# A planner's price for transfers: one rate for the whole run, and a later due time for the rows of x in the output stage

## The chip, the cores and the metric

The kernel runs on one core of a Trainium2 chip. The metric is the time of one execution on the device in microseconds (us), lower is better. Three runs of the kernel before gave 2049.25, 2057.58 and 2060.75 us; their median, 2057.58 us, is the time before.

## What is computed

One layer of a streaming encoder runs over 2048 prompt frames and, with caches, over 32 sample frames; the model width D is 1024. Two branches read the same normalised rows h: A is attention over a band of nine chunks of 64 frames (8 heads of 64), B is a gated delta rule (8 heads of 64) in its exact chunked form. Cut to what matters:

```python
h = layer_norm(x, ln0_g, ln0_b)
qa, ka, va, za, qkv_b, zb, a_b, b_b, gate_a, gate_b = split(h @ w_in)      # 1024 x 6160
oa = softmax(qa @ band(ka).T * 64**-0.5 + rel_bias) @ band(va)
ya = (oa * silu(za)) @ w_branch_a
c  = silu(causal_conv(qkv_b, conv_w))                                      # width 4
q, k, v = l2norm(c_q) * 64**-0.5, l2norm(c_k), c_v
g, beta = -exp(a_log) * softplus(a_b + dt_bias), sigmoid(b_b)
# per head and chunk of 64 frames, with decay from cumsum(g):
M = strict_lower((beta * k) @ k.T * decay);  T = inverse(I + M)
u, w = T @ (beta * v), T @ (beta * k * exp(gc))
v_new = u - w @ S;  o = (q * exp(gc)) @ S + (q @ k.T * decay) @ v_new
S = S * exp(g_last) + (k * exp(g_last - gc)).T @ v_new                     # chunk after chunk
yb = (rms_norm(o) * gdn_norm_w * silu(zb)) @ w_branch_b
mix = sigmoid(gate_a) * ya + sigmoid(gate_b) * yb
y = layer_norm(2**0.25 * h + mix @ w_out, ln_g, ln_b)
```

The last keys and values, the last three rows before the convolution and the state S are outputs too. Wide products are made exact enough by splitting each operand into a high and a low part and adding three products (high by high, low by high, high by low).

## The kernel before

**Stages.** The prompt is worked in two halves of 1024 frames (the sample frames ride with the second). Per half, phase B (delta rule) comes first, then phase A (attention). Under both runs one stream of projection jobs: one job is 128 columns of `w_in` times all frames of the half, and its matmuls write the PSUM tile `pj`. The jobs fill TensorE between the short dependent matmuls of the phases. When the second half's jobs are used up, a last stage multiplies the gated branch outputs (`glo`, `ghi`) by the branch weights (PSUM tile `a`, three banks), multiplies by the gate rows (`sg`, read back from `sig`), adds the branches, splits the sum into `mh` and `ml`, multiplies by `w_out` (`woh`, `wol`; PSUM tiles `pj` and `b`), adds a row block of x (`xt`), and normalises. That stage goes through eight blocks of 256 frames.

**The delta rule's solve.** A system is eight chunks of one pair of heads; there are 17. Its matrix leaves as `sol_p<-p_c` (four transfers), comes back spread as `sys_p<-sol_p` (four), VectorE solves it by substitution in 62 short instructions on `sys_t` and `sys_u`, the result leaves as `sol_u<-sys_u` (four), comes back as `tu<-sol_u`, VectorE transposes it (`tu_t`), and TensorE completes the inverse (`b<-tu_t,p_c`). After that the recurrence runs on TensorE and VectorE in turn (`x<-state,k_bd`, `r`, `x<-r,u_bd`, `vn`, `x<-vn,kd_bd`, `state`).

**What sets the order.** The program is written by a planner that runs while the kernel is built. Each piece of work is a Python generator (a stream) with its own clock. `Flow.run` always advances the stream with the smallest clock, and each instruction that a stream issues adds a price (`Engine.price`) to that clock and to its engine's. The order in which the planner issues is the order of the instructions on each engine, and on the chip each engine keeps that order. All transfers are issued by SyncE (SP), in that same order. The planner prices a transfer in `Flow.transfer` (line 204): the issue takes 0.5 us, data moves one transfer after another through a single resource `"DMA"` at `size / rate`, and 1.6 us (`MARGIN`) is added. A stream that yields the returned time goes on only when the planner's clock has got there. So the price of a transfer decides how far down each engine's queue its first user stands; on the chip that user still waits for the real landing. The rate is 360e3 bytes per us for transfers that start before the planner's 25 us, and 200e3 after that. Sizes are counted with at least 768 bytes for each contiguous run (line 291).

**Lines of the steps.** `transfer` 204 to 211, `dma` 283 to 292, `solve` 1255, `inverse` 1291, `last_weights` 2006 (loads of `w_out`, each started 5 us, `LEAD`, before the landing planned for the one before), `load_g` 2071 (`glo`), `merge` 2093, `sg_ahead` 2189, `x_load` 2212, `finish` 2230. Nearly every recorded instruction has line 262, the wrapper's; its tiles tell which it is.

Of the kernel before, what the change touches and what calls it, by code (L numbers as in the profile page):

```python
# [21 lines left out]
P = 128  # L22
# [133 lines left out]
class Flow:  # L156
# [47 lines left out]
    def transfer(self, queue, size):  # L204

        start = max(self.cur.clock + 0.2, self.busy.get(queue, 0.0)) + 0.5
        self.busy[queue] = start

        end = max(start + 0.6, self.busy.get("DMA", 0.0)) + size / (360e3 if start < 25.0 else 200e3)
        self.busy["DMA"] = end  # L210
        return end + MARGIN

# [58 lines left out]
def trunk(ctx: ExitStack, tc: tile.TileContext, x_p, x_s, cache_k, cache_v, st_conv, st_gdn,  # L271
# [11 lines left out]
    def dma(dst, src, eng=nc.sync):  # L283

        eng.dma_start(dst, src)  # L285
        size = 2 if dst.dtype == F16 else 4
        n = size
        for k in dst.shape:
            n *= k

        n = max(n, n // (size * dst.shape[-1]) * 768)
        return flow.transfer("SP" if eng is nc.sync else "S", n)
# [7 lines left out]
    def mark():  # L300
        return Mark(flow)
# [1902 lines left out]
    def x_ahead():  # L2204
        n = SEQ // P
        for gt in [*range(n - 2), n, n - 2, n - 1]:
            yield x_slots
            w = Rows()
            flow.start(x_load(w, gt, P if gt < SEQ // P else DEC))
            q_x[gt == SEQ // P].put(w)  # L2210

    def x_load(w, gt, rows):
        w.ready, w.half_done = mark(), mark()
        w.xt = xt = fp.tile([P, D], F32, tag="xt", bufs=3, name="xt")
        w.st = fp.tile([P, 2, 6], F32, tag="fst", bufs=3, name="fst")
        yield dma(xt[:rows], x_s if rows < P else x_p[gt * P:(gt + 1) * P, :])
        yield rows_ready
        V.tensor_scalar(out=xt[:rows], in0=xt[:rows], scalar1=mv[:rows, gt, 0:1],
                        scalar2=mv[:rows, gt, 1:2], op0=ALU.subtract, op1=ALU.mult)
        yield  # L2220
        eng = V if gt < 2 else G

        for name, op in (("l0g", ALU.mult), ("l0b", ALU.add)):
            for q in range(4):
                cs = slice(q * 256, (q + 1) * 256)
                eng.tensor_tensor(out=xt[:rows, cs], in0=xt[:rows, cs], in1=rowv[name][:rows, cs], op=op)
            yield
        w.ready.done()
# [130 lines left out]
```

## Time and profile before

| | |
|---|---|
| runs | 2049.25, 2057.58, 2060.75 us |
| profiled execution | 2061.14 us, of which the span of the instructions is 2059.3 us |
| mean granted clock of TensorE | 0.983 of full speed |
| TensorE matmuls busy | 1977.9 us, 96% of the span |
| VectorE, ScalarE, GpSimd busy | 1454.2, 976.6, 711.3 us |
| transfers | 196.55 MB, mean 95 GB/s |

Busy time is the time in which at least one instruction of the engine is recorded as running. Phase B of the first half lies at about 100 to 480 us, phase A at 480 to 800, the second half's phase B at 900 to 1290 and phase A at 1290 to 1655. At 1655 to 1750 the projections end and the output stage begins; from 1750 to 2000 it runs evenly.

### The profile page before, as it was taken

How to read it: one execution, taken by the hardware profiler on the slowest of the kernel's cores; microseconds unless marked ns; L12 is line 12 of the kernel's file. 1: busy time of each engine (PE TensorE's matmuls, PEld its weight loads, DVE VectorE, ACT ScalarE, POOL GpSimd, SP SyncE). 2: the span in 40 equal slices, each digit the busy share in tenths (PEclk: the TensorE clock that was granted, in tenths of full speed). 3: DMA queues.
4: the chain of work that ended last, by engine and by line, in shares of the span. 5: the costliest groups of instructions: out<-in, count | busy, mean ns of one | idle time of the engine just before them, and what ended most of it. 6: DMA issues, size and time to landing. Idle time of an engine off the chain costs nothing. (4 is left out here: it accounts for less than half of the span.)

```text
span 2059.3 us, 42008 instructions
## 1 busy us (share of the span) xinstructions
PE 1977.9 (96%) x15157; PEld 1422.6 (69%) x15157; DVE 1454.2 (71%) x4674; ACT 976.6 (47%) x2098; POOL 711.3 (35%) x1075
## 2 busy tenths in 40 slices
PE   8999999999999998998999999999999998999998
PEld 5455666666466656565767777766776687999996
DVE  7788888773478757679988886356757677655665
ACT  6665455444466667564544544356656551111110
POOL 6444343333312123344243442311111134643453
PEclk9999999999999999999999999999999999999999
DMA  4223332332333233223232233332233355433331
GB/s 139 65 85 108 94 89 71 84 104 80 112 90 116 68 94 89 66 81 84 66 80 78 78 104 86 105 92 75 75 95 92 94 161 179 135 103 122 104 125 47
DMA packets 198745, 196.55 MB, mean 95 GB/s; under 512 B 80642, under 2 KB 148590, under 8 KB 198536
## 3 DMA queue, kind: packets, MB, share of 16 engines
q1 hardware_dynamic: 198536, 193.86, 32.0%
q8 instruction: 120, 1.97, 0.4%
q14 instruction: 89, 0.73, 0.1%
HBM read 135.91 MB, written 50.53 MB: 91 GB/s over the span
## 5 line engine op out<-in xcount | busy, mean ns | idle before, releaser
L262 PE MATMUL pj<-hi,whi 128*128 128x512 f16 (+2 forms) x1992 | 649.9, 341 | 11.9 <-ACT sig L262 3.2
L262 PE MATMUL pj<-hi,wlo 128*128 128x512 f16 (+2 forms) x1952 | 641.7, 341 | 0.5 <-POOL wlo L262 0.5
L262 PEld LDWEIGHTS <-whi 128*128 128x128 f16 x3984 | 412.3, 105 | 212.9 <-issue 8.3
L262 PE MATMUL pj<-lo,whi 128*128 128x512 f16 (+2 forms) x1992 | 459.9, 338 | 0.0
L262 POOL TENSOR_TENSOR wlo<-wraw,whi 128x256 f16<-128x256 f32 x384 | 265.1, 712 | 555.5 <-ACT whi L262 305.5
L262 PEld LDWEIGHTS <-wlo 128*128 128x128 f16 x1952 | 206.3, 106 | 113.6 <-issue 11.2
L262 ACT CAST mh<-sg 128x256 fp32r<-128x256 f32 x64 | 26.0, 407 | 275.4 <-DVE sg L262 275.4
L262 ACT ACTIVATE wraw<-wraw,w_scale 128x1024 f32<-128x1024 f32 (+1 forms) x98 | 111.6, 1139 | 58.5 <-DVE w_scale L262 54.3
L262 PE MATMUL a<-ghi,whi 128*128 128x256 f32 (+1 forms) x512 | 132.3, 289 | 6.8 <-DVE sg L262 6.6
L262 ACT CAST ph<-b 128x512 f16<-128x512 f32 (+2 forms) x224 | 92.6, 422 | 91.9 <-PE b L262 87.0
L262 PE MATMUL a<-ghi,wlo 128*128 128x256 f32 (+1 forms) x512 | 130.5, 286 | 1.1 <-DVE wlo L262 1.1
L262 DVE TENSOR_TENSOR sys_u<-sys_u,sys_t 128x60 f32<-128x60 f32 (+23 forms) x527 | 125.5, 242 | 7.8
L262 ACT CAST whi<-wraw 128x512 f16<-128x512 f32 (+1 forms) x196 | 119.3, 611 | 24.2 <-PE pj L262 21.4
L262 DVE TENSOR_TENSOR pl<-b,ph 128x512 f16<-128x512 f32 (+2 forms) x224 | 106.8, 484 | 30.4 <-ACT ph L262 29.3
L262 ACT ACTIVATE sb<-sb,mx,unit 128x640 f32<-128x640 f32 (+4 forms) x128 | 108.9, 851 | 22.9 <-DVE mx L262 22.4
L262 DVE SCALAR_TENSOR_TENSOR acc<-raw,cwT,acc 128x512 f32<-128x512 f32 x144 | 113.5, 789 | 7.7 <-ACT acc L262 6.5
L262 DVE TENSOR_TENSOR sys_t<-sys_u,sys_p 128x60 f32<-128x60 f32 (+21 forms) x459 | 111.0, 243 | 6.5
L262 POOL TENSOR_TENSOR w_scale<-w_scale,mhalf 128x1 f32<-128x1 f32 x49 | 30.0, 612 | 245.2 <-DVE w_scale L262 181.0
L262 ACT COPY v_t<-o 128x64 f32<-128x64 f32 x132 | 27.6, 209 | 163.4 <-PE o L262 124.2
L262 PEld LDWEIGHTS a<-ghi,whi 128*128 128x128 f32 x512 | 97.9, 191 | 9.2 <-DVE sg L262 8.8
L262 PE MATMUL b<-ident,sb 128*128 128x128 f32 x560 | 99.4, 277 | 2.5 <-DVE ga L262 1.4
L262 DVE CUSTOM_DVE_ANT_0 sb<-a,bias 128x320 f32<-128x320 f32 (+4 forms) x128 | 61.7, 486 | 54.2 <-PE a L262 53.7
(353 smaller groups left out, 4288.8 us busy)
## 6 DMA issues: line engine op xcount, KB each, us to landing
wraw<-in_w_in SPq DMA_DIRECT2D x192, 256.0 KB
sg<-sig SPq DMA_DIRECT2D x112, 128.0 KB
sig<-sig SPq DMA_DIRECT2D x44, 256.0 KB
sys_p<-sol_p SPq DMA_DIRECT2D x68, 128.0 KB
x<-in_x_p SPq DMA_DIRECT2D x16, 512.0 KB
xt<-in_x_p SPq DMA_DIRECT2D x16, 512.0 KB
out_y_p<-xt SPq DMA_DIRECT2D x16, 512.0 KB
glo<-g SPq DMA_DIRECT2D x14, 512.0 KB
```

Of the source, the lines that this page charges most:

```text
L262: r = f(*a, **k)
```

## The change

Two edits. `Flow.transfer` counts every transfer at 360e3 bytes per us, whenever it starts. `x_load` adds 3.0 us to the planned landing of each row block of x, before its first use. Every engine keeps the same number of instructions; what changes is their order.

```diff
--- before.py
+++ after.py
@@ -206,7 +206,7 @@
         start = max(self.cur.clock + 0.2, self.busy.get(queue, 0.0)) + 0.5
         self.busy[queue] = start
 
-        end = max(start + 0.6, self.busy.get("DMA", 0.0)) + size / (360e3 if start < 25.0 else 200e3)
+        end = max(start + 0.6, self.busy.get("DMA", 0.0)) + size / 360e3
         self.busy["DMA"] = end
         return end + MARGIN
 
@@ -2213,7 +2213,8 @@
         w.ready, w.half_done = mark(), mark()
         w.xt = xt = fp.tile([P, D], F32, tag="xt", bufs=3, name="xt")
         w.st = fp.tile([P, 2, 6], F32, tag="fst", bufs=3, name="fst")
-        yield dma(xt[:rows], x_s if rows < P else x_p[gt * P:(gt + 1) * P, :])
+
+        yield dma(xt[:rows], x_s if rows < P else x_p[gt * P:(gt + 1) * P, :]) + 3.0
         yield rows_ready
         V.tensor_scalar(out=xt[:rows], in0=xt[:rows], scalar1=mv[:rows, gt, 0:1],
                         scalar2=mv[:rows, gt, 1:2], op0=ALU.subtract, op1=ALU.mult)
```

**VectorE, the first solve of the run.** `tu_t<-tu` opens the inverse of the first system; the rows on `sys_t` and `sys_u` are the substitution of the second one, and the last number of their shape falls by one from step to step. Before:

```order
L262 TENSOR_TENSOR sys_t<-sys_u,sys_p 128x4x18
L262 RECIPROCAL w_half<-w_scale 128x1
L262 TENSOR_TENSOR qk_bd_739<-b,e_in 64x4x64 x2
L262 SCALAR_TENSOR_TENSOR acc<-raw_2128,cwT,acc 128x512
L262 TENSOR_TENSOR sys_u<-sys_u,sys_t 128x4x18
L262 TENSOR_SCALAR w_inv<-w_half,h_scale 128x1
L262 TENSOR_SCALAR w_half<-w_half,h_scale 128x1
L262 STREAM_TRANSPOSE tu_t<-tu 128x256
L262 TENSOR_TENSOR sys_t<-sys_u,sys_p 128x4x17
```

After:

```order
L262 TENSOR_TENSOR sys_t<-sys_u,sys_p 128x5x15
L262 TENSOR_SCALAR w_scale<-w_scale 128x1
L262 TENSOR_TENSOR p_c_768<-b,gcb 128x256
L262 TENSOR_TENSOR sys_u<-sys_u,sys_t 128x5x15
L262 RECIPROCAL w_half<-w_scale 128x1
L262 STREAM_TRANSPOSE tu_t<-tu 128x256
L262 TENSOR_TENSOR qk_bd_739<-b,e_in 64x4x64 x2
L262 TENSOR_TENSOR sys_t<-sys_u,sys_p 128x5x14
```

The second system's substitution is three steps further along where the first system's result is taken up. On TensorE the first `b<-tu_t,p_c` stands 60 matmuls earlier in the program than before (the 893rd and not the 953rd), and the later ones of the first half 71 to 133 earlier.

**SyncE, where the output stage begins.** `l0g`, `l0b`, `lng`, `lnb` are the vectors of the two norms spread over 128 partitions (512 KB each) when they come from `in_ln`, and buffers for pieces of `w_out` when they come from `in_w_out`. `xt` is 512 KB of x, `glo` the gated outputs of block 1, `sg<-sig` gate rows (here `sig_74`, `sig_75`, `sig_82`, `sig_83` belong to block 0, the others to block 1). Before:

```order
L285 DMA glo<-g_66 128x4x256
L285 DMA glo<-g_67 128x4x256
L285 DMA lng<-in_w_out 128x512
L285 DMA sg<-sig_69 128x256
L285 DMA sg<-sig_77 128x256
L285 DMA sg<-sig_70 128x256
L285 DMA sg<-sig_78 128x256
L285 DMA lng<-in_w_out 128x512
L285 DMA l0g<-in_ln_g 128x1024
L285 DMA l0b<-in_ln_b 128x1024
L285 DMA xt<-in_x_p 128x1024 x3
L285 DMA lng<-in_ln_g 128x1024
```

After:

```order
L285 DMA sg<-sig_74 128x256
L285 DMA l0g<-in_ln_g 128x1024
L285 DMA sg<-sig_82 128x256
L285 DMA l0b<-in_ln_b 128x1024
L285 DMA sg<-sig_75 128x256
L285 DMA xt<-in_x_p 128x1024 x2
L285 DMA sg<-sig_83 128x256
L285 DMA xt<-in_x_p 128x1024
L285 DMA lng<-in_ln_g 128x1024
L285 DMA glo<-g_66 128x4x256
L285 DMA glo<-g_67 128x4x256
L285 DMA sg<-sig_68 128x256
```

The norm's vectors and the rows of x have moved ahead of everything of block 1, and in between the last gate rows of block 0.

**VectorE at the same place.** `xt<-xt,mv` is the first use of a row block of x, `glo<-glo,ghi` the split of block 1's input, `sg<-sg,a` empties a bank of `a`. Before:

```order
L262 TENSOR_TENSOR glo<-glo,ghi 128x256 x4
L262 TENSOR_TENSOR wol_22609<-lng,woh_22588 128x512
L262 TENSOR_SCALAR xt<-xt,mv 128x1024
L262 TENSOR_TENSOR xt<-xt,l0g 128x256 x4
L262 TENSOR_SCALAR xt<-xt,mv 128x1024
L262 TENSOR_TENSOR xt<-xt,l0b 128x256 x4
L262 TENSOR_TENSOR xt<-xt,l0g 128x256 x4
L262 TENSOR_SCALAR xt<-xt,mv 128x1024
L262 SCALAR_TENSOR_TENSOR xt<-pj,xt 128x512
```

After:

```order
L262 SCALAR_TENSOR_TENSOR sg<-sg,a 128x256 x2
L262 TENSOR_TENSOR sg<-sg 128x256
L262 TENSOR_SCALAR xt<-xt,mv 128x1024
L262 TENSOR_TENSOR xt<-xt,l0g 128x256 x4
L262 TENSOR_SCALAR xt<-xt,mv 128x1024
L262 TENSOR_TENSOR xt<-xt,l0b 128x256 x4
L262 TENSOR_SCALAR xt<-xt,mv 128x1024
L262 TENSOR_TENSOR xt<-xt,l0g 128x256 x4
L262 TENSOR_TENSOR glo<-glo,ghi 128x256 x2
L262 SCALAR_TENSOR_TENSOR xt<-pj,xt 128x512
L262 TENSOR_TENSOR glo<-glo,ghi 128x256 x2
```

The split of block 1's input has moved from before the rows of x to behind them. The two passes `xt<-xt,m,lng` and `xt<-xt,m,lnb` of the first row block, which stood behind block 1's first `sg<-sg,a`, now stand ahead of it.

## Rows read from the trace of the kernel before

**Rows 1.** The page: the span, and busy time by engine.

```profile
span 2059.3 us, 42008 instructions
PE 1977.9 (96%) x15157; PEld 1422.6 (69%) x15157; DVE 1454.2 (71%) x4674; ACT 976.6 (47%) x2098; POOL 711.3 (35%) x1075
```

**Rows 2.** Windows: stretch, busy PE, PEld, DVE, ACT, POOL (count), clock, DMA share, GB/s.

```profile
100.00:480.00 380.00, 364.29 (x2641) 238.65 (x2639) 312.95 (x1147) 194.03 (x386) 148.66 (x250) 0.97 0.33 91
...
800.00:900.00 100.00, 92.02 (x721) 64.03 (x722) 68.06 (x141) 61.01 (x117) 39.37 (x63) 0.97 0.22 68
900.00:1290.00 390.00, 374.56 (x3210) 281.32 (x3209) 326.84 (x1187) 181.83 (x406) 143.37 (x254) 0.98 0.30 83
...
1655.00:1750.00 95.00, 85.01 (x617) 75.35 (x615) 70.20 (x150) 30.28 (x68) 39.58 (x39) 0.95 0.53 170
1750.00:2000.00 250.00, 250.00 (x1578) 227.20 (x1577) 147.62 (x276) 33.18 (x91) 115.67 (x148) 1.00 0.37 116
```

**Rows 3.** Waits of PE: total us, times, longest.

```profile
PE a L262 <- DVE sg L262: 6.6, 7, 2.3
...
PE x L262 <- DVE state L262: 4.0, 8, 0.9
PE x L262 <- DVE r L262: 3.7, 12, 0.7
PE x L262 <- DVE vn L262: 3.4, 9, 1.1
...
PE x L262 <- DVE sys_t L262: 2.8, 2, 2.3
```

**Rows 4.** Timeline of SP, first solve (start us, us, engine, line, op, tiles).

```profile
124.77 1.85 SPq L285 DMA_DIRECT2D sys_p<-sol_p  x4
...
177.59 0.51 SPq L285 DMA_DIRECT2D tu<-sol_u  x1
```

**Rows 5.** Tile sys_p and timeline of DVE: first uses in the first solve.

```profile
L262 DVE TENSOR_SCALAR sys_t<-sys_p,sys_u x68: 221/240/687, 135.0 to 1244.7; 128x31 f32<-128x31 f32 x17, 128x30 f32<-128x30 f32 x17, 128x29 f32<-128x29 f32 x17, 128x28 f32<-128x28 f32 x17
...
197.56 0.43 DVE L262 STREAM_TRANSPOSE tu_t<-tu 128x256 f32<-128x256 f32 x1
```

**Rows 6.** Timeline of SP at the start of the output stage.

```profile
1703.27 0.96 SPq L285 DMA_DIRECT2D l0g<-in_ln_g  x1
1704.27 0.44 SPq L285 DMA_DIRECT2D l0b<-in_ln_b  x1
1704.75 1.64 SPq L285 DMA_DIRECT2D xt<-in_x_p  x3
```

**Rows 7.** Timeline of DVE there; in brackets idle time before, and what ended it.

```profile
1702.58 3.42 DVE L262 TENSOR_TENSOR glo<-glo,ghi 128x256 fp32r<-128x256 f32 x4
...
1712.98 0.81 DVE L262 TENSOR_SCALAR xt<-xt,mv 128x1024 f32<-128x1024 f32 x1 [5.26 <-DMA xt<-in_x_p]
...
1727.14 0.41 DVE L262 SCALAR_TENSOR_TENSOR sg<-sg,a 128x256 f32<-128x256 f32 x1
...
1728.07 1.27 DVE L262 SCALAR_TENSOR_TENSOR xt<-xt,m,lng 128x1024 f32<-128x1024 f32 x1
```

**Rows 8.** Timeline of PE there.

```profile
1727.60 0.39 PE L262 MATMUL a<-ghi,whi 128*128 128x256 f32 x1 [2.32 <-DVE sg L262]
...
1744.92 0.39 PE L262 MATMUL a<-ghi,whi 128*128 128x256 f32 x1 [1.42 <-DVE sg L262]
```

**Rows 9.** The chain of waits: start us, us, what.

```profile
1704.75 8.14 DMA xt<-in_x_p
...
1749.46 5.48 PE pj L262 x24
...
1771.30 22.77 PE a L262 x192
```

**Rows 10.** Windows of 10 us at the start of the output stage.

```profile
1670.00:1680.00 10.00, 8.84 (x52) 7.49 (x52) 6.28 (x16) 3.23 (x7) 2.50 (x2) 0.56 0.46 152
...
1700.00:1710.00 10.00, 8.34 (x35) 6.38 (x36) 5.59 (x7) 5.18 (x13) 5.95 (x7) 1.00 0.93 276
```

## The prediction

> **What bounds the kernel now.** I read the page first. The span is 2059.3 us and TensorE's matmuls are recorded busy for 1977.9 of them [rows 1]; every other engine is busy for less than three quarters. So the end is set by TensorE's stream of work, and a change of order can only move what TensorE loses: time without a matmul, and time at the lower of its two clock levels. Next comes the table of busy time by stretch [rows 2]. It shows where the losses sit: TensorE idles 380 - 364.29 = 15.7 us in the first half's phase B, 390 - 374.56 = 15.4 us in the second's, 8.0 us between the halves (800 to 900) and 10.0 us where the output stage begins (1655 to 1750); from 1750 to 2000 it idles not at all. The granted clock in the four stretches is 0.97, 0.98, 0.97 and 0.95. Half speed is the lower level, so a mean of 0.97 over 380 us means 0.03 x 380 = 11.4 us of lost full-speed time; in the same way 7.8, 3.0 and 4.8 us for the others. All together 49.1 us idle and 27.0 us of clock. The third view, TensorE's waits by releaser [rows 3], names what it waits for: no transfer at all, mostly VectorE, in pieces of a few us.
>
> **What the change moves.** No instruction comes or goes, so the sum has three terms, one for each place where the order differs, and one for the rest.
>
> *The solves of the delta rule.* By the text of the planner, a system's four transfers are counted as follows: `sol_p` and `sol_u` go in runs of 128 bytes, each counted as 768, so four times 196.6 KB, and `tu` as 786 KB too; `sys_p` is four times 131 KB. At 200e3 that is 3.93 + 2.62 + 3.93 + 3.93 = 14.4 us, at 360e3 8.0 us. Each of the 17 systems is thus planned 6.4 us shorter, and its matmuls stand 60 to 133 places earlier among the projections in the first half. Does the data come in time? In the trace, the first system's `sys_p` is issued from 124.77 to 126.6 and first used at 135.0, 8.4 us later; `tu` is issued at 177.59 and first used at 197.56, 20 us later [rows 4, 5]. The uses come later than the plan by more than what the plan now loses, so VectorE should still find its data there, at least in this system, and the earlier place costs nothing; it hides behind VectorE's own backlog (312.95 of 380 us busy [rows 2]). What may it give? An upper bound is everything that the recurrence waits for on VectorE, 4.0 + 3.7 + 3.4 + 2.8 = 13.9 us [rows 3], and the two stretches' clock loss with it, 11.4 + 7.8: -33 us. The other end is the same waits once more, +13.9 us, should TensorE now meet the recurrence before VectorE has got there. I take -2 us, by the row nearest to the edit: 2.8 us in two waits that end on `sys_t`, a matmul held up by a substitution running late.
>
> *The start of the output stage.* Now VectorE stands 5.26 us at the first row of x, until 1712.98; then it works through the first output rows and empties the first bank of `a` of block 1 at 1727.14, and TensorE has idled 2.32 us for it, and 1.42 us for a later one [rows 7, 8]. The x rows are issued at 1704.75 behind `l0g` and `l0b`, and the first is 8.14 us under way [rows 6, 9]. In the new order `l0g` goes out ahead of the last three gate rows of block 0. Each of these feeds a group of twelve matmuls, 22.77 / 16 = 1.42 us [rows 9], so the rows of x go out some 4.3 us earlier at the least, landing near 1708.6, if the queue is as deep as now. VectorE gets there earlier as well, since the split of block 1's input (3.42 us) is no longer ahead of it. But that split, and two passes of 1.27 us each [rows 7], now stand between the first row of x and the first emptied bank: 3.42 + 2.54 = 6.0 us more. Net 6.0 - 4.3 = 1.7 us later at the least gain; if x lands 9 us earlier, as it could when nothing but VectorE's own queue holds it, 3 us sooner. I take -1 us. Lower end: both gaps gone, -3.7 us. Upper end: 1.7 us from this sum, and the last gate row of block 0, which now lies behind 4 x 524 KB and with the gate rows 2.5 MB in all. At the 276 GB/s that the fullest 10 us show [rows 10] these take 9.0 us, against four groups, 5.7 us, until TensorE needs it: 3.3 us late, of which the first output bank's earlier matmuls can hide all (it needs the last piece after 14 of its 24, 14/24 x 5.48 = 3.2 us [rows 9]) or none. So +5.0 us.
>
> The row just used speaks against the rate itself: 276 GB/s at a DMA share of 0.93 [rows 10] leaves no room for 360. The Trainium skill, page "DMA: Bandwidth & Descriptors", section Specifications, gives about 358 GB/s as a core's limit at HBM, which would make the new rate right even in a full queue; the trace does not agree here. By the page's figure the 2.5 MB would take 7.0 us (an estimate), the last gate row would be late by 1.3 us and wholly hidden, and the term's upper end would be 1.7 us.
>
> *The 3 us for rows of x.* In the even part of the output stage TensorE is busy for 250.00 of 250 us [rows 2]; a later place of `xt<-xt,mv` on VectorE, which is busy for 147.62 there, is hidden by that. Taken at 0. Without that cover one bank would wait, 1.42 us per block.
>
> *The rest.* Between the halves and in the attention phases nearly every stream is dealt out anew, with no side that the profile favours: 0, with the 8.0 us idle and 3.0 us of clock between the halves as the size of what could go or come again, so 11 either way.
>
> The sum is -2 - 1 = -3 us against the profiled execution's own 2061.14 us (span 2059.3 and 1.84 around it), so 2058.1. That execution lay 3.6 us over the median of the runs, 2057.58; the forecast for the median is 2057.58 - 3, rounded down: 2054 us, no change that could be measured.
>
> **Rivals.** *The plan is now nearer to the chip, and many small losses go.* For it: small transfers land long before their first use (20 us for `tu`), so the old rate only held work back, and TensorE's idle time is 49.1 us in dozens of pieces, with 27.0 us of clock behind them; one 10 us stretch at a mean clock of 0.56 cost 4.4 us alone [rows 10]. Against it: VectorE does the same work in these stretches. If a quarter of both goes: 76.1 / 4 = 19 us, so 2038.5 us.
>
> *The planner now believes in more than the DMA engines deliver, and queues stand at transfers that have not landed.* This is the slower one. Its place is VectorE at `sys_p`: the plan of that step shrinks by 2.62 - 1.46 = 1.16 us, with no short runs counted double in it, so there the old rate may have been right. For it: the 276 GB/s of [rows 10], and the 5.26 us that VectorE stood at x even with the old rate [rows 7]. Against it: the first system's 8.4 us in hand. Price: 17 x 1.16 = 19.7 us of VectorE, of which half comes through to TensorE (VectorE idles 16 to 18% of these stretches), 9.9 us, with 5.0 us at the output stage: +15, so 2072.5 us. It decides from the point where the waits of VectorE at `sys_p` come to more than about 0.6 us a system, and matmuls of the recurrence begin to wait for VectorE longer than now.
>
> *The order changes and nothing else does.* TensorE then loses as much as now at other places: 2057.6 us. For it: matmul work is the same and 96% of the span. This falls in the same band as the forecast.
>
> **How the numbers follow.** No change (the forecast with the third rival) 0.45, the faster rival 0.33, the slower 0.22. About 0.5%, 10.3 us, is what a measurement of this kernel can tell from no change, its runs being 11.5 us apart. The forecast's own range is 2047 to 2065; since the two others hold more than half of the chance, the range takes in both of their times and leaves out only the outer ends of the terms: 2035 to 2073. Faster by over 0.5% (below 2047.3) 0.33, within 0.45, slower (above 2067.9) 0.22.
>
> **What would show it.** Right on the solves: `tu_t<-tu` starting within some 15 us of its issue, VectorE waiting for no `sys_p`, TensorE's idle time in phase B within a few us of 15.7 and 15.4. Right on the output stage: VectorE's wait at the first row of x under 2 us, and TensorE's gap before the second bank of block 1 between 0 and 4 us. Wrong: waits of VectorE or ScalarE that end on a transfer and come to over 10 us in phase B (slower rival), or a granted clock of 0.99 and more with under 10 us idle in either phase B (faster rival), or a difference that sits in the attention phases, which I have counted at nothing.

## The result

Each comparison ran the two kernels in turn on the same chip.

| | before | after |
|---|---|---|
| median of the runs | 2058.68 us (2049.25 to 2063.13, 10 runs) | 2045.89 us (2041.47 to 2048.63, 10 runs) |
| ratio, 95% interval | | 0.9937 [0.9926, 0.9948] |

The changed kernel is faster by 0.63%, 12.8 us: more than the 0.5% that I had set as the bound for no change. The time lies in the predicted range, but the likeliest case (no change, 2054) is not the one that came. What came is the faster case, to which I had given 0.33; 2045.89 lies 1 us outside the forecast's own range (2047 to 2065), and inside the wide one only because that was opened for the rivals.

The page of the kernel after, and the mean clock, against [rows 1]:

```profile
span 2046.2 us, 42039 instructions
PE 1972.3 (96%) x15157; PEld 1416.8 (69%) x15157; DVE 1450.2 (71%) x4674; ACT 980.5 (48%) x2098; POOL 712.0 (35%) x1075
```
```profile
core 0: 2046.2 us, clock 0.986
```

Idle TensorE time fell from 2059.3 - 1977.9 = 81.4 us to 73.9, and what the lower clock level costs (one minus the mean clock, times the span) from 0.017 x 2059.3 = 35.0 us to 28.6. What is left after both is 1942.9 us before and 1943.7 after: the same work, to within the rounding of the clock. So the difference of the two spans, 13.1 us, is 7.5 us less idling and 6.4 us less clock, less these 0.8 us. The counts of the five engines are those of before; the 31 instructions more in the total are not among them.

The windows of the kernel after, in the columns of [rows 2]:

```profile
100.00:480.00 380.00, 365.33 (x2692) 242.07 (x2691) 312.38 (x1172) 194.44 (x392) 150.23 (x253) 0.98 0.33 91
...
800.00:900.00 100.00, 95.61 (x718) 64.58 (x717) 67.21 (x133) 63.36 (x117) 41.30 (x70) 0.98 0.21 64
900.00:1290.00 390.00, 376.64 (x3248) 282.74 (x3247) 328.92 (x1218) 181.34 (x409) 147.47 (x256) 0.98 0.31 82
...
1655.00:1750.00 95.00, 88.30 (x572) 78.96 (x572) 74.35 (x131) 25.35 (x56) 50.64 (x53) 0.96 0.58 190
1750.00:2000.00 250.00, 248.41 (x1617) 228.31 (x1617) 154.54 (x283) 32.39 (x90) 114.65 (x147) 1.00 0.38 117
```

No stretch stands out. Idle time went from 15.7 to 14.7 us in the first phase B, from 8.0 to 4.4 between the halves, from 15.4 to 13.4 in the second phase B, from 10.0 to 6.7 where the output stage begins; in the two attention phases together it changed by 0.3 us. The clock rose by 0.01 in three of the stretches. TensorE's waits, in the columns of [rows 3], are again many small ones, and none ends on a transfer:

```profile
PE a L262 <- DVE sg L262: 5.3, 4, 2.1
PE x L262 <- DVE vn L262: 4.7, 12, 0.8
...
PE x L262 <- DVE r L262: 4.0, 11, 1.1
...
PE x L262 <- DVE sys_u L262: 1.9, 2, 1.1
```

The first solve, in the timelines of SyncE and of VectorE, and the tile `sys_p` with the heading under it ([rows 4, 5]):

```profile
125.67 1.85 SPq L285 DMA_DIRECT2D sys_p<-sol_p  x4
...
180.89 0.38 SPq L285 DMA_DIRECT2D tu<-sol_u  x1
```
```profile
188.75 0.43 DVE L262 STREAM_TRANSPOSE tu_t<-tu 128x256 f32<-128x256 f32 x1
```
```profile
L262 DVE TENSOR_SCALAR sys_t<-sys_p,sys_u x68: 220/237/720, 131.4 to 1221.0; 128x31 f32<-128x31 f32 x17, 128x30 f32<-128x30 f32 x17, 128x29 f32<-128x29 f32 x17, 128x28 f32<-128x28 f32 x17
its engine sat idle before it (us, times) until:
```

`tu` is taken up 7.9 us after its issue and not 20. The heading "sat idle before it" has nothing under it: VectorE never waited for `sys_p`.

The start of the output stage, on SyncE, VectorE and in TensorE's timeline and the chain ([rows 6 to 9]):

```profile
1680.55 1.70 SPq L285 DMA_DIRECT2D xt<-in_x_p  x2
```
```profile
1688.58 0.42 DVE L262 SCALAR_TENSOR_TENSOR sg<-sg,a 128x256 f32<-128x256 f32 x1 [0.94 <-DMA sg<-sig]
1689.04 0.42 DVE L262 TENSOR_TENSOR sg<-sg 128x256 f32<-128x256 f32 x1
1689.38 0.81 DVE L262 TENSOR_SCALAR xt<-xt,mv 128x1024 f32<-128x1024 f32 x1
```
```profile
1684.31 0.39 PE L262 MATMUL a<-ghi,whi 128*128 128x256 f32 x1 [2.14 <-DVE sg L262]
```
```profile
1709.49 22.77 PE a L262 x192
```

VectorE's wait of 5.26 us at the first row of x is gone. The last sum of block 0 (`sg<-sg`, 1689.04) stands just ahead of the x rows; this pair matters below. Block 1 runs through its 192 matmuls without a gap. But part of what went there came again in block 0, to which the gap of 2.14 us belongs. TensorE's waits for an emptied bank in the window 1655 to 1750, before and after:

```profile
PE a L262 <- DVE sg L262: 5.2, 6, 2.3
```
```profile
PE a L262 <- DVE sg L262: 3.7, 3, 2.1
```

### The profile page after: what moved, and what is told of

It is laid out like the page before. It is cut to its first block, busy times and chain, and to the rows that moved or that the text cites. A ratio compares the mean times of both kernels' runs of the same rounds, so it can differ in the third digit from the quotient of the medians.

```text
span 2046.2 us, 42039 instructions
## 1 busy us (share of the span) xinstructions
PE 1972.3 (96%) x15157; PEld 1416.8 (69%) x15157; DVE 1450.2 (71%) x4674; ACT 980.5 (48%) x2098; POOL 712.0 (35%) x1075
## 4 chain that ended last, share of the span: by engine, by line
PE 68%; DVE 17%; issue 4%; ACT 4%; POOL 3%; DMA 2%; SPq 1%; POOLq 0%; DVEq 0%; ACTq 0%
PE pj L262 37%; PE b L262 13%; PE a L262 10%; PE x L262 3%; PE c L262 2%; DVE acc L262 2%; DVE sys_t L262 2%; DVE sys_u L262 2%; PE o L262 2%; POOL wlo L262 1%; DVE kd_bd L262 1%; SPq L285 1%; DVE q_bd L262 1%; ACT whi L262 1%; ACT wraw L262 1%
## 5 line engine op out<-in xcount | busy, mean ns | idle before, releaser
L262 PEld LDWEIGHTS <-wlo 128*128 128x128 f16 x1952 | 205.6, 105 | 111.6 <-issue 10.8
L262 DVE TENSOR_TENSOR sys_u<-sys_u,sys_t 128x60 f32<-128x60 f32 (+24 forms) x527 | 124.5, 242 | 5.7
L262 PEld LDWEIGHTS a<-ghi,wlo 128*128 128x128 f32 x512 | 97.4, 190 | 2.5 <-DVE wlo L262 1.8
```

The costliest lines, as they stand in the source:

```text
L262: r = f(*a, **k)
```

## The experiments

Times are medians; ratios are to the kernel before on the same chip (2056.9 to 2057.6 us).

| kernel | us | ratio, 95% interval |
|---|---|---|
| rate alone | 2064.31 | 1.0036 [1.0023, 1.0049] |
| 3.0 us alone | 2055.72 | 0.9992 [0.9983, 1.0002] |
| 350e3, with 3.0 us | 2043.03 | 0.9931 [0.9919, 0.9942] |
| 205e3, without | 2050.55 | 0.9969 [0.9957, 0.9981] |
| 360e3 until the output stage | 2044.93 | 0.9939 [0.9919, 0.9959] |
| 360e3 in the output stage | 2074.82 | 1.0082 [1.0064, 1.0101] |
| 360e3, x after the last sum | 2048.48 | 0.9956 [0.9941, 0.9971] |
| 1000e3, with 3.0 us | 2046.28 | 0.9947 [0.9931, 0.9962] |
| 360e3 for the solves | 2043.34 | 0.9936 [0.9922, 0.9950] |
| 360e3 for the rest | 2035.86 | 0.9901 [0.9885, 0.9917] |
| 195e3, without | 2063.66 | 1.0035 [1.0022, 1.0049] |
| after, 2.5 us on the bias | 2056.65 | 0.9999 [0.9986, 1.0013] |

Two questions were put: which part of the change acts, and whether the rate acts by being nearer to the chip (theory 1) or by drawing another order (theory 2).

**The two edits apart.** The first kernel is the one after without the 3.0 us:

```diff
-        yield dma(xt[:rows], ...) + 3.0
+        yield dma(xt[:rows], ...)
```

> The new rate for the whole run, without the 3.0 us for rows of x. TensorE has the same order as the changed kernel; VectorE, GpSimd and SyncE differ only in the output stage. The kernel before is at about 2058.5 us, the changed one at 2046. Theory 1 (a rate near what small transfers take lets many small losses go) and theory 2 (any new rate redraws nearly the whole order, and this draw happens to lose less): the gain is all in the rate, so 2046 us, within 2 us of the changed kernel. Theory 3 (the later due time of the rows of x gives it, in the output stage): 2056 to 2059 us.

The second is the kernel before with the 3.0 us:

> The old rates, with the 3.0 us for rows of x alone. TensorE's order is that of the kernel before but for a few rows in the output stage, so all that differs lies after 1700 us. Theories 1 and 2: within 2 us of the kernel before, 2057 to 2060 us. Theory 3: 2046 to 2050 us; VectorE's wait of 5.26 us at the first row of x must then be gone, and TensorE's gaps of 2.32 and 1.42 us with it, which can give 3.7 us and not 12.

Neither edit by itself gives the gain. The rate alone makes the kernel slower by 0.36%, which no theory had; the 3.0 us alone are worth nothing measurable, so theory 3 falls. Against the kernel after, the rate alone loses 20 us (1.0036 - 0.9937 of 2057), and its trace shows where. TensorE, at its first output bank, has two gaps that the kernel after does not have:

```profile
1693.05 0.79 PE L262 MATMUL pj<-woh,mh 128*128 128x512 f32 x1 [8.09 <-ACT mh L262]
...
1701.36 0.80 PE L262 MATMUL pj<-woh,ml 128*128 128x512 f32 x1 [4.61 <-POOL ml L262]
```

What those two wait for runs from VectorE's last sum of block 0 over ScalarE's `mh` to GpSimd's `ml`. The three engines' timelines:

```profile
1683.83 0.81 DVE L262 TENSOR_SCALAR xt<-xt,mv 128x1024 f32<-128x1024 f32 x1 [0.43 <-DMA xt<-in_x_p]
...
1687.08 1.42 DVE L262 TENSOR_TENSOR xt<-xt,l0b 128x256 f32<-128x256 f32 x4
...
1690.48 0.42 DVE L262 TENSOR_TENSOR sg<-sg 128x256 f32<-128x256 f32 x1
...
1692.02 3.56 DVE L262 TENSOR_TENSOR xt<-xt,l0b 128x256 f32<-128x256 f32 x4
```
```profile
1689.88 1.32 ACT L262 CAST ghi<-glo 128x256 fp32r<-128x256 f32 x4 [6.31 <-DMA glo<-g]
1691.37 1.32 ACT L262 CAST ghi<-glo 128x256 fp32r<-128x256 f32 x4 [0.17 <-DMA glo<-g]
1692.60 0.40 ACT L262 CAST mh<-sg 128x256 fp32r<-128x256 f32 x1
```
```profile
1689.36 5.07 POOL L262 TENSOR_TENSOR xt<-xt,l0g 128x256 f32<-128x256 f32 x4 [8.53 <-issue]
1694.39 3.52 POOL L262 TENSOR_TENSOR glo<-glo,ghi 128x256 fp32r<-128x256 f32 x4
1697.87 2.75 POOL L262 TENSOR_TENSOR xt<-xt,l0b 128x256 f32<-128x256 f32 x4
1700.59 0.72 POOL L262 TENSOR_TENSOR ml<-sg,mh 128x256 fp32r<-128x256 f32 x1
```

On each of them other work stands ahead: on VectorE the passes over x (from 1683.83 until the sum at 1690.48), on ScalarE the casts of block 1's input, for which it waits 6.31 us, on GpSimd 11.2 us on the third row block and block 1. With the 3.0 us all three engines take the last sum's chain first (VectorE at 1689.04 and 1689.38, above). So at the first rows of x the margin does not cover a late landing (VectorE waited 0.43 us for the first); it moves x behind work that TensorE needs. The two gaps are 12.7 us. The windows of the same kernel show what came with them:

```profile
1655.00:1750.00 95.00, 75.78 (x465) 67.95 (x466) 62.28 (x107) 21.90 (x49) 48.64 (x49) 0.91 0.52 172
1750.00:2000.00 250.00, 243.82 (x1537) 220.83 (x1536) 151.34 (x269) 31.45 (x86) 114.62 (x136) 1.00 0.34 110
```

Against after, the first window has 12.5 us more idle time and 0.05 x 95 = 4.8 us more lost clock, the second 4.6 us more idle time: 21.9 us. The two spans lie only 14.5 us apart, since the profiled execution of the rate alone had the highest mean clock of its seven (0.988, the others from 0.983) and that of after (0.986) one under the mean of its ten, 0.988.

From this came theory 4: the new rate saves some 11 us before the output stage; in that stage, by itself, it costs some 16; the 3.0 us take the cost away.

**The rate by stage.** Both without the 3.0 us; `last` is set when the output stage's first stream starts (shortened here, against the line of after, as are the rate edits below):

```diff
-  end = max(...) + size / 360e3
+  end = max(...) + size / (360e3 if start < 25.0 else 200e3 if self.last else 360e3)
```

> 360e3 until the output stage's first stream starts, 200e3 from there on, and no 3.0 us: the phases are planned as in the changed kernel, the output stage as in the kernel before. Theory 4, formed after the run with the rate alone: the new rate saves about 11 us before the output stage (the projections ended at 1645.3 and not at 1655.6 us), and in the output stage alone it costs some 16 us, because the passes over the first rows of x come on VectorE ahead of the last sum of block 0 for which TensorE waits; the 3.0 us put them behind it. Then this kernel has the gain without the cost: 2043 to 2049 us. Rival A (rate and margin only work together, and the phases give nothing by themselves): 2055 us or more. Rival B (the phases' gain is chance and differs with each order): this order is that of the changed kernel up to the output stage, so 2046 us also.

and with the two rates exchanged:

> 200e3 until the output stage's first stream starts, 360e3 from there on, and no 3.0 us: the phases as in the kernel before, the output stage as with the rate alone. Theory 4: the cost without the gain, 2057 + 16 = 2073 us, 2068 to 2077, with TensorE idle for 8 and 5 us in its first output bank (for ScalarE's mh and for GpSimd's ml). Rival A: within 3 us of the kernel before, 2054 to 2060 us. Rival C (what was lost with the rate alone is a wait for transfers that a fuller queue makes late, and the queue is fuller only where the phases end earlier): 2057 to 2063 us.

Both came as theory 4 said: 2044.93 and 2074.82 us. The first alone gives all of the change's gain (0.9939 against 0.9937), the second gives the cost alone, +17 us, at a later place in time and with the same two waits:

```profile
1708.40 0.80 PE L262 MATMUL pj<-woh,mh 128*128 128x512 f32 x1 [6.09 <-ACT mh L262]
...
1716.60 0.79 PE L262 MATMUL pj<-woh,ml 128*128 128x512 f32 x1 [3.99 <-POOL ml L262]
```

Rivals A and C fall. Rival B, that the gain in the phases is chance, expected the same as theory 4 of the first kernel and is still open here.

**The place, without the 3.0 us.** The first three row blocks wait for a mark that the last sum sets:

```diff
         yield rows_ready
+        if gt < 3:
+            yield fold_done
         V.tensor_scalar(out=xt[:rows], ...
```

> 360e3 for the whole run, no 3.0 us; the first three row blocks of x wait in the plan for the last sum of block 0's branches instead, so their passes stand behind it on VectorE whatever the planned landing is. Theory 4 (the place behind the sum is all that the 3.0 us give): within 3 us of the changed kernel, 2043 to 2049 us, and TensorE without its waits of 8 and 5 us. Rival D (the 3.0 us help because the data lands later than planned, at each of the 17 row blocks): only the first part of the loss goes, 2052 to 2062 us, with VectorE's waits at later rows of x still there.

2048.48 us, inside theory 4's interval, though by the ratios 4 us from after and not within 3 (the two intervals overlap). TensorE's matmuls stand in the same order in this kernel, with the rate alone and in after, so the other engines' orders make the difference. TensorE's waits (window 1655 to 1850) name no `mh` and no `ml`:

```profile
PE a L262 <- DVE sg L262: 6.5, 6, 2.1
```

So the place behind the sum is most of what the 3.0 us give, 16 of the 20 us by the ratios. The other 4 sit at later rows. Between 1750 and 2000, TensorE's waits in this kernel and in after are

```profile
PE a L262 <- DVE sg L262: 6.1, 5, 1.3
```
```profile
PE a L262 <- DVE sg L262: 1.6, 1, 1.6
```

and with the rate alone 6.2 us in five again. Ahead of each of the five here, VectorE waits for a gate row:

```profile
1859.29 1.50 DVE L262 SCALAR_TENSOR_TENSOR sg<-sg,a 128x256 f32<-128x256 f32 x3 [1.61 <-DMA sg<-sig]
```
```profile
1859.76 0.39 PE L262 MATMUL a<-ghi,whi 128*128 128x256 f32 x1 [1.18 <-DVE sg L262]
```

SyncE sends the row of x ahead of this gap behind a group of two gate rows (x at 1853.00, the next gate rows from 1857.15); in after it goes out behind a group of six. So rival D holds in part: its time did not come, but VectorE's waits at later rows of x are there (3.5 us in five, none in after), and what they leave over is late gate rows.

**How much is the rate, how much the draw.** The rate after 25 us was set to other values: 350e3 and 1000e3 with the 3.0 us, 205e3 and 195e3 without.

```diff
-  size / 360e3
+  size / (360e3 if start < 25.0 else 350e3)
```

> The changed kernel with 350e3 bytes per us after 25 us in place of 360e3: 3% less, but four fifths of TensorE's rows stand in another order than in the changed kernel. Theory 1: a plan nearly as near to the chip, so 2045 to 2049 us. Theory 2: a new draw, anywhere from 2042 to 2066 us; more than 5 us away from the changed kernel speaks for it. Theory 3: 2046 us.

> The changed kernel with 1000e3 bytes per us after 25 us in place of 360e3, with the 3.0 us: the plan now counts transfers as almost nothing but their fixed part. VectorE has the passes over x behind the last sum, as in the changed kernel. Theory 1 (nearness to the chip gives the gain): the plan is off on the other side, engines meet transfers that have not landed, and the time goes back up, 2052 to 2065 us. Rival E (shorter is better: the plan loses by holding work back, and too early a place costs little since other streams cover it): 2040 to 2047 us. Theory 2 (each new order is a new draw): anywhere from 2042 to 2066 us.

> The kernel before with 205e3 bytes per us after 25 us in place of 200e3, and no 3.0 us: 2.5% more, with well over half of TensorE's rows in another order. Theory 1: the plan is hardly nearer to the chip, so 2056 to 2060 us. Theory 2: a new draw, anywhere from 2042 to 2066 us; a time more than 5 us from the kernel before, either way, speaks for it. Theory 3: 2058 us.

> The kernel before with 195e3 bytes per us after 25 us in place of 200e3, and no 3.0 us. 205e3 gave 2050.6 us, 6.4 less than 200e3. Theory 2 (a small change of the rate draws a new order, and the one at 200e3 is unlucky by some 6 us or more): 2045 to 2054 us, faster than before although the rate moves away from the good ones. Theory 1 in its steep form (the time falls with the rate, most of it near 200e3): 2060 to 2066 us. A flat curve with one lucky order at 205e3: 2056 to 2060 us.

350e3 gave 2043.03, 2 us under theory 1's interval; it is 1.2 us from after by the ratios, so theory 2's sign, more than 5 us, did not come. 1000e3 gave 2046.28, though no row here shows such a rate: theory 1 would have it slower, rival E (holding work back costs, early costs little) expected it. 205e3 gave -6.4 us, outside theory 1 and inside theory 2. 195e3 gave +6.3: so the order at 200e3 is not an unlucky one, as theory 2 had it there, and only the steep curve expected this. By that curve, 6.4 us for 5e3, 210e3 would give all that 360e3 gives, and nothing more would come from there to 1000e3. A curve of that shape and chance look alike on so few points, so the change was split another way.

**The rate by kind of transfer**, before the output stage, with 200e3 in it:

```diff
-  size / 360e3
+  size / (360e3 if start < 25.0 else 200e3 if self.last else 360e3 if solve else 200e3)
```

> 360e3 for the four transfers of each solve alone (sol_p, sys_p, sol_u, tu), before the output stage; 200e3 for all else after 25 us; no 3.0 us. With 360e3 for all transfers before the output stage it was 2044.9 us against 2057.6 for the kernel before, so 12.7 us are to be shared out. Theory S (the solves, moved to an earlier place among the projections, give the gain): 2044 to 2050 us. Theory O (the gain comes from the other transfers): 2055 to 2059 us. Theory 2 (the old order is an unlucky one, and nearly any other loses less): 2044 to 2052 us as well, together with the kernel that has 360e3 for the other transfers alone.

and the other way round:

> The counterpart: 200e3 for the solves' transfers, 360e3 for all others before the output stage, 200e3 in it, no 3.0 us. Theory S: 2055 to 2059 us. Theory O: 2044 to 2050 us. Theory 2: 2044 to 2052 us, here and with the solves alone, so that the two gains together are more than the 12.7 us.

The solves alone gave -14.0 us, the rest alone -21.5, both together -12.7. The parts do not add up: their sum would be -35.5. Theories S and O fall, each expecting one of the two at 2055 us or more; theory 2, that each split is a new draw, expected two gains that are too large together, but put both at 2044 us or more, 0.7 and 8 us too high. Rival E does not account for the second either: with the solves' transfers back at the longer price it is 8 us faster, by the ratios, than with 360e3 for all. The second is the fastest kernel of the study, 0.9901 against after's 0.9937, with intervals that do not meet. Its page and clock:

```profile
span 2032.3 us, 42014 instructions
PE 1960.9 (96%) x15157; PEld 1409.9 (69%) x15157; DVE 1443.0 (71%) x4674; ACT 979.5 (48%) x2098; POOL 712.0 (35%) x1075
```
```profile
core 0: 2032.3 us, clock 0.991
```

Idle 71.4 us, clock 0.009 x 2032.3 = 18.3, and the same rest, 1942.6 us. In this execution it wins more by the clock (16.7 us against before) than by idling (10.0). Every execution has a mean clock of its own, and over all six of them the clock is 11.7 of the 20.1 us by which the mean span is shorter. The solves alone win by the clock almost only: 12.3 of 12.9 us (0.990 on the mean against 0.984). In their trace the two phases B idle as long as before, 31.4 us against 31.1, at a clock higher by 0.01:

```profile
100.00:480.00 380.00, 361.46 (x2691) 241.25 (x2690) 313.83 (x1171) 194.00 (x390) 155.21 (x252) 0.98 0.33 91
...
900.00:1290.00 390.00, 377.16 (x3269) 283.45 (x3268) 327.85 (x1199) 182.33 (x411) 143.45 (x248) 0.99 0.31 84
```

350e3 is alike, 12.5 of 13.3 us. So what one order has over another is to a large part the clock, which TensorE's waits do not show. Why these orders keep it up where the others lose it was not found.

**A visible wait taken away.** In the kernel after VectorE waits for the loads of the attention's bias; its waits for them are

```profile
DVE bias L262 <- DMA bias<-ext_dram: 10.9, 5, 4.0
```

```diff
-  yield dma(b[:], ...)
+  yield dma(b[:], ...) + 2.5
```

> The changed kernel with 2.5 us added to the planned landing of each 327 KB load of the attention's bias, at which VectorE waits 10.9 us in 5 waits (up to 4.0) in the changed kernel. If these waits reach TensorE, those in the attention phases go: 2040 to 2044 us. If VectorE has them to spare there (it is busy for 60 to 63% of these stretches): 2044 to 2048 us. By theory 2 the new order alone moves it by up to some 5 us either way.

2056.65 us, slower by 10.8 than after (12.8 by the ratios): outside each interval, and more than twice what theory 2 allowed for. The edit does what it says: of VectorE's waits on transfers these remain, and no bias among them,

```profile
DVE sg L262 <- DMA sg<-sig: 9.6, 5, 3.8
...
DVE st L262 <- DMA x<-in_x_p: 3.8, 2, 2.0
```

but from 547 us on TensorE's matmuls stand in another order than in after, and TensorE idles 2054.7 - 1972.8 = 81.9 us, 8.0 more than after:

```profile
span 2054.7 us, 42059 instructions
PE 1972.8 (96%) x15157; PEld 1415.0 (69%) x15157; DVE 1449.0 (71%) x4674; ACT 980.0 (48%) x2098; POOL 713.6 (35%) x1075
```

## Why the prediction was right and wrong

*The bound* was right. TensorE's work is about 1943 us in the kernels for which the sum is shown, and the span is that plus its idling and its clock. Over all fourteen traces the work comes out between 1936.6 and 1946.1 us, so the sum closes to some 6 us and not better.

*Place by place*, in the windows shown for before and after (us; the windows are fixed in time, so work near an end can fall into the next one, and the clock is rounded to 0.01, which is up to 2 us in one phase B):

| place | foretold | idle | clock |
|---|---|---|---|
| the two phases B | -2 | -3.1 | -3.8 |
| between the halves | 0 within 11 | -3.6 | -1.0 |
| attention phases | 0, with the row above | -0.3 | 0 |
| 1655 to 1750 | -1 | -3.3 | -1.0 |
| 1750 to 2000 | 0 | +1.6 | 0 |

The phases B, the time between the halves and the start of the output stage all came out faster than foretold, and none of the values has the clock in it, though two of the bounds had. That is where -3 fell short of -12.8.

*The solves, -2 us.* The readings of the place were right: `tu` taken up within 15 us, no wait for `sys_p`, idle time of 14.7 and 13.4 us in the two phases B, all as foretold. The slower rival's place shows no wait, so it is refuted there. The size was not right, and 2.8 us of waits was the wrong row for it: 360e3 for the solves alone measured -14.0 us, within the bounds of -33 to +13.9, and almost all of it is the clock and not a wait. How much of it belongs to the solves is open, since that edit changes the order of nearly the whole run.

*The start of the output stage, -1 us.* Right in size. VectorE's 5.26 us at x are gone, and no gap stands before block 1's second bank. Both of block 1's gaps went, which was my lower end of -3.7, but new ones came in block 0, so TensorE's waits for a bank fell by 1.5 us only: that they meet -1 is in part luck. After against the kernel with 360e3 only before that stage measures 0.9937 to 0.9939, nothing, but the intervals would also allow 4 us. The late gate row that made the upper end cost VectorE 0.94 us. I had taken 276 GB/s as what the queues deliver, from one window of one order. The fullest 10 us by rate in after, and in the kernel with 350e3, are

```profile
1680.00:1690.00 10.00, 7.44 (x37) 6.32 (x37) 7.57 (x14) 5.33 (x9) 3.69 (x4) 0.83 0.94 323
```
```profile
1680.00:1690.00 10.00, 7.58 (x42) 6.18 (x41) 7.74 (x13) 4.21 (x7) 3.96 (x4) 1.00 1.01 369
```

323 GB/s at a share of 0.94, and 369 at 1.01 (so the count over 10 us is off by a per cent or more). The Trainium skill, page "DMA: Bandwidth & Descriptors", section Specifications, gives about 358 GB/s as a core's limit at HBM. I wrote that the trace does not agree; the second row does, to 3%. So 276 GB/s was no ceiling, and my sentence that it leaves no room for 360 was wrong.

*The 3 us for rows of x, 0.* This step failed. With the old rate it holds (0.9992). With the new rate it is 20 us, of which 16 sit at the first rows and some 4 at later ones. I asked what a later place of x costs, saw it hidden by a TensorE that is never idle from 1750 on, and did not ask what an earlier place costs, just before: the rate alone puts x ahead of block 0's last sum and of the `mh` and `ml` made from it, on the path that sets the end. I had read the order only with both edits in it, where the one edit had already repaired the other.

*The rest, 0 within 11.* By place it held: -4.6 us between the halves, next to nothing in the attention phases. By kind of transfer the picture is another one: 360e3 for all but the solves, before the output stage, measured -21.5 us, and with the solves -12.7. The two parts make -35.5 us apart and -12.7 together, so what an order gives cannot be added up from terms by place, and the sum had no way to see it.

*The rivals.* The first foretold that a quarter of 76.1 us goes. In the four stretches 15.7 us went (idle 49.1 to 39.2, clock 27.0 to 21.2), a fifth; the other stretches took 2.6 of it back. Its amount was nearly right. Of its reasons, a plan nearer to the chip was not borne out, as 1000e3 does as well. The other one, that the old rate held work back, agrees with 1000e3, 205e3 and 195e3, not with the kernel that has the solves' transfers back at 200e3 and is the fastest. Shown is that two orders of the same work can lie 13 us apart (195e3 and 205e3) or 1 (350e3 and 360e3). Among the runs with an intact output stage, those with 350e3 or more, for all transfers or for some, give 2035.9 to 2048.5 us, save one at 2056.7; those at 195e3 to 205e3 give 2050.6 to 2063.7. That a higher rate is better on the mean is likely from these, but they are too few to call it shown, and which property of an order decides stays open.

## What to carry to other kernels

Where a planner writes the order, a changed price has two effects: the local one, which can be read from the trace, and a redraw of everything else, which here is worth anything from 1 to some 13 us and has to be measured over several prices before one of them is called better. Look at the mean clock as well as at the waits: here it is half or more of what several orders gain. Build the two halves of a change apart and read the order of each; here one half was needed only to repair the other. And a wait of an engine that does not set the time (10.9 us of VectorE) can be taken away and the kernel still be slower.

## Not expected of the hardware

VectorE's four passes `xt<-xt,l0b` took 1.42 us at 1687.08 and 3.56 us at 1692.02, when GpSimd was at work on the same kind of passes (rows of the rate alone, above), and GpSimd's own four passes took between 2.75 and 5.07 us. All fourteen traces agree. The four passes over a row block of x (`xt<-xt,l0g` or `xt<-xt,l0b`) took VectorE 1.42 or 1.43 us in all 26 places where GpSimd did nothing. In 13 of the 17 places with GpSimd at work for over four fifths of the time they took 3.37 to 3.60 us; in the other four VectorE kept 1.42 or 1.43, and GpSimd's passes were the slow ones (four in 5.07 us, three in 6.31). So the price of a pass depends on what the other engine does, by a factor of up to 2.5, and the planner has one price for it. The Trainium skill, page "SBUF — State Buffer", section "SBUF: two separate sides", says that a VectorE operation with two SBUF inputs and a GpSimd operation that reads SBUF take one pair of ports in turn, the later one blocked. The traces agree in that one of the two is slow; no run here moved these passes to test it.
